# A hybrid layer and a 32-expert mixture on one core: TensorE's order in the expert loop fixed by issue edges, the last norm's weights loaded

## The chip, the cores and the metric

The kernel runs on one core of a Trainium2 chip. The time is device microseconds of one execution, from its start to its end; the time before is the median of three runs. One further execution was taken by the hardware profiler, and all rows below come from it. TensorE multiplies (PE: its matmuls, PEld: its weight loads), VectorE is DVE, ScalarE is ACT, GpSimd is POOL, and SyncE (SP) issues the transfers.

## The reference, cut to what matters

Two blocks over 256 tokens of width 1024. The first mixes four branches (three attentions and a convolution) and ends in a gated feed-forward; the second has a pooling and differential-attention mixer, cross attention and a mixture of experts. Only the last stage is touched by the change in more than a detail:

```python
def clamped_swiglu(gu):
    gate, up = gu[..., :D_EXPERT], gu[..., D_EXPERT:]
    gate = jnp.minimum(gate, SWIGLU_LIMIT)
    up = jnp.clip(up, -SWIGLU_LIMIT, SWIGLU_LIMIT)
    return (up + 1.0) * gate * jax.nn.sigmoid(SWIGLU_ALPHA * gate)

def moe_ffn(...):        # 256 tokens, 32 experts, each token to its best 4
    logits = (xt @ w_router + b_router).astype(jnp.float32)
    top_val, top_idx = lax.top_k(logits, TOP_K)
    gates = jax.nn.softmax(top_val, axis=-1)
    ...
        hb = clamped_swiglu(xb @ w_gu[e] + b_gu[e])    # w_gu[e]: 1024 x 2048
        yb = hb @ w_down[e] + b_down[e]                # w_down[e]: 1024 x 1024
        return yb * g[:, None].astype(yb.dtype)
    ...
    y = jnp.zeros((T, D), h.dtype).at[row_tok].add(...)

x = x + moe_ffn(rms_norm(x, ffn_norm_g[l]), ...)
return rms_norm(x, final_norm_g)
```

All is float32. Every expert's weights are read once: 8 MiB of `w_gu` and 4 MiB of `w_down`, 384 MiB in all.

## The kernel before

The first 750 us or so compute everything up to the router; the rest is a loop over 32 experts (`NE`), each with room for 64 tokens (`CAP`). An expert that got more tokens is finished by `overflow()`, a run-time branch (`tc.If`) whose body is skipped when no expert has more than 64.

**Slots.** The expert weights stream through 24 buffers of 128 x 2048 floats (`slot_tile()`, taken in turn). A slab is one transfer of 1 MiB into one slot: an expert has 8 slabs of gate/up weights (`load_gu`) and 4 of down weights (`load_dn`). All are issued on SP's queue in the order of use; a slot's next load waits until TensorE has used the slot, and also for an earlier transfer. The last slab of expert 31 comes in two halves.

**One expert on TensorE.** `front(e)` runs `gu_product`: the 64 gathered tokens times 8 slabs, into two PSUM banks (`gue`, tag mm, line 1513), 8 records a slab in the trace. `gu_out` copies them to `gs` (ScalarE, line 1521). `swiglu` turns `gs` in two halves, `make(0)` and `make(1)`, each 4 transposes (`gte`, line 1534) and then six operations on VectorE and one on ScalarE, into `u_`. `dn_product` multiplies `u_` by 4 slabs (`dne`, tag y, line 1560, 8 records a slab) and splits the sum into `yh` and `yl` (ScalarE line 209, VectorE line 210), scaled by the slot's gate. `slots_of` makes the one-hot tile `Se` on VectorE and turns it on TensorE (`ste`, lines 1432 and 1433) into `sT`. `scatter` adds the rows to the tokens' sums with 8 matmuls (`acc`, line 1570), which stay in four PSUM banks through the loop. Every second expert `gather` picks the tokens of the next two (`xgg`, line 1460, 32 records) with a selection tile `SXg` from VectorE, and VectorE copies them out (line 1462).

**The order.** The loop is skewed: in iteration e the gate/up product of e + 1 runs, then the down product of e. The small pieces are handed in as `between`, a table from k (the step of the product ahead of which the call stands) to functions. In `gu_product` k counts slabs, in `dn_product` half slabs. That position is only the place in the program text: a scheduler orders the instructions of each engine by their dependences, and may move small matmuls among the large ones. Edges of issue (`tc.issue_after`, wrapped in `behind`) forbid this where they are given; the products have none.

**The end.** `EOVER` is 29: in that iteration all weights of 30 and 31 that are left are issued, since SP's queue must not stop at the branch. Behind the branch (line 1607) stand the spreading of the last norm's weights over the partitions (`gb2`, 16 records of line 1669), the swiglu of expert 30, the products gate/up 31, down 30 and down 31, the last scatters, and `finish`, which scales and stores the result.

Of the kernel before, what the change touches and what calls it, by code (L numbers as in the profile page):

```python
# [22 lines left out]
P = 128  # L23
T = 256
D = 1024
# [18 lines left out]
def kernel(ctx: ExitStack, tc: tile.TileContext, A, out, probe=None, stop=None):  # L44
# [45 lines left out]
    def ps(name, tag="mm"):  # L90
        return pst["pool"].tile([P, 512], F32, tag=tag, name=name, bufs=pst["tags"][tag])
# [400 lines left out]
    def attention(name, qk, kchunk, vcol, bias, sink=None, extra=None, cq=None):  # L492
# [3 lines left out]
        for p in range(4):  # L496
# [36 lines left out]
            for j in range(2):  # L533
                ptr = ps(f"{name}t{p}{j}", "tr")
                for b in (1, 0):
# [3 lines left out]
                    for s in range(b + 1):  # L539
# [28 lines left out]
    v5 = load_vecs("v5", [("attn", r128(A["attn_norm_g_2"]), 8), ("xattn", r128(A["xattn_norm_g_2"]), 8),  # L568
                     ("memn", r128(A["mem_norm_g_2"]), 8), ("ffn", r128(A["ffn_norm_g_2"]), 8),
                     ("pscale", r128(A["pool_scale_2"]), 4), ("subln", A["subln_g_2"], 1),  # L570
                     ("fgattn", A["final_g"].rearrange("(c p) -> c p", p=P), 8),
                     ("last", A["final_norm_g_2"].rearrange("(c p) -> c p", p=P), 8)])


    qc = qk_group("foxqk", 1792, 8, 4)
# [916 lines left out]
    def load_gu(src, ahead=()):  # L1492
        return [*ahead, *(gu_piece(src, k, slot_tile()) for k in range(len(ahead), 8))].__getitem__
# [10 lines left out]
    def gu_product(wt, xg, col, name, between=None):  # L1504

        pgu = [ps(f"gu{name}_{n}") for n in range(2)]
        for k in range(8):
            for f in (between or {}).get(k, ()):
                f()
            w = wt(k)  # L1510
            for n in range(2):
                for cg in range(2):
                    PE.matmul(pgu[n][cg * CAP:(cg + 1) * CAP, :], xg[:, k, col:col + CAP],  # L1513
                              w[:, cg * D + n * 512:cg * D + (n + 1) * 512], start=k == 0, stop=k == 7)
        return pgu
# [35 lines left out]
    def dn_product(wt, gslot, name, u_=u_, tag="y", between=None):  # L1551

        po = ps(f"dn{name}", tag)
        for k in range(8):
            for f in (between or {}).get(k, ()):
                f()
            if k % 2 == 0:
                w = wt(k // 2)
            for cg in range(2):
                PE.matmul(po[cg * CAP:(cg + 1) * CAP, :], u_[:, k // 4, k % 4, :],  # L1560
                          w[:, k % 2, cg * 512:(cg + 1) * 512], start=k == 0, stop=k == 7)
        hilo(yh, yl, po, scale=gslot() if callable(gslot) else gslot)

    def scatter(stop=False, after=None):
# [20 lines left out]

    def front(e, between):
        w = load_gu(w_gu[e], () if e else gu0)
        pgu = gu_product(w, st["xg"], (e % GR) * CAP, f"e{e}", between)

        return gu_out(pgu, f"e{e}", slot_tile()[:, :D] if e == EOVER + 1 else None)  # L1590

    def slots_of(e):
        st["gslot", e] = turn_slots(one_hot(pos1[:, :, e:e + 1], 1, f"e{e}")[:, :, 0], gate3[:, :, e, :], f"e{e}")
# [8 lines left out]

    def overflow():
        wsl = [slot_tile() for _ in range(2)]
        oxg = slot_tile()[:, :D // 2].rearrange("p (c s) -> p c s", c=8)
# [29 lines left out]

    for e in range(NE - 2):
        make = swiglu(gs, bgu[:, :, e], f"e{e}")
        make(0)
        between = {1: [lambda: make(1, "y")], 4: [lambda: slots_of(e)]}
        if e and e - 1 != EOVER:  # L1640
            between[3] = [scatter]
        gs = front(e + 1, between)
        wd = load_dn(w_dn2[e])
        if e == 15:
            load_b_down()
        if e == EOVER:

            wg1 = load_gu(w_gu[e1])
            wd0, wd1 = load_dn(w_dn2[e0]), load_dn(w_dn2[e1], halves=True)
        if e == 2:  # L1650
            counts()
        between = {}
        if e % GR == 0:
            _, four = group(e // GR + 1)
            between = {0: [lambda: four(0)], 4: [lambda: four(1)]}
        if e == 15:
            between = {4: [gates_down], 6: [add_b_down]}
        dn_product(wd, st["gslot", e], f"e{e}", between=between)

    scatter()  # L1660
    overflow()


    work = slot_tile()
    gb2 = work[:, D:]
    for h in range(2):
        pt = ps(f"gb2_{h}")
        for c in range(4):
            PE.matmul(pt[:, c * P:(c + 1) * P], vec["last"][:, 4 * h + c:4 * h + c + 1].to_broadcast([P, P]), ident,  # L1669
                      start=True, stop=True)  # L1670
        S.copy(gb2[:, half(h)], pt)
    make = swiglu(gs, bgu[:, :, e0], f"e{e0}")
    make(0)
    slots_of(e0)
    gs = gu_out(gu_product(wg1, st["xg"], (e1 % GR) * CAP, f"e{e1}", {1: [lambda: make(1)]}), f"e{e1}")
    u1 = slot_tile()[:, :2 * 4 * CAP].rearrange("p (h c s) -> p h c s", h=2, c=4)
    make1 = swiglu(gs, bgu[:, :, e1], f"e{e1}", u1)
    dn_product(wd0, st["gslot", e0], f"e{e0}", between={2: [lambda: make1(0)], 4: [lambda: make1(1)]})
    dn_product(wd1, lambda: st["gslot", e1], f"e{e1}", u_=u1, tag="mm",
               between={2: [scatter], 4: [lambda: slots_of(e1)]})  # L1680
    ssl = mp.tile([P, 3, 2], F32, name="ssl")
# [49 lines left out]
```

## Time and profile before

| | |
|---|---|
| median of three runs | 1711.93 us (1711.44 to 1714.88) |
| the profiled execution | 1709.1 us |
| its span, first to last instruction | 1707.4 us |
| TensorE matmuls busy | 1621.0 us, 95% |
| weight loads / VectorE / ScalarE / GpSimd busy | 59% / 42% / 30% / 13% |
| read from HBM | 524.95 MB |

The page cuts the span into 40 slices of 42.7 us and gives each engine's busy share in tenths. A busy TensorE is not one at its peak, since matmuls overlap and their ends are modelled; how long a record takes in a run is better read from the starts of neighbouring rows in the timeline. A wait is put down to the event that ended it.

### The profile page before, as it was taken

The page shows a single profiled execution, that of the slowest core. Times are in us where ns is not written, and L with a number is a line of the kernel's source. Part 1 is how long each engine was busy: PE and PEld are TensorE (multiplying, and loading weights), DVE is VectorE, ACT ScalarE, POOL GpSimd, SP SyncE. Part 2 cuts the span into 40 slices and gives each one's busy share as a digit, 9 for nine tenths or more (in the row PEclk, how much of TensorE's full clock was granted, in tenths as well). Part 3 has the DMA queues.
Part 4 walks back from the last instruction along what each step waited for, and adds up shares of the span by engine and source line. Part 5 has one row for each costly group of instructions (what it writes and reads, how often), then busy time and mean ns, then how long its engine had stood idle before and what let it go on. Part 6 is the DMA issues. An engine that isn't in the chain of part 4 may idle for free. (4 is left out here: it accounts for less than half of the span.)

```text
span 1707.4 us, 23465 instructions
## 1 busy us (share of the span) xinstructions
PE 1621.0 (95%) x9269; PEld 1002.7 (59%) x9270; DVE 722.7 (42%) x1613; ACT 510.5 (30%) x959; POOL 221.2 (13%) x319
## 2 busy tenths in 40 slices
PE   9899999999999999999999999999999999999977
PEld 8887799989999888974333333333333333333332
DVE  5967654667777776542222212212121212122212
ACT  4465554555555555531110111001011110010101
POOL 6988412200011000000000000000000000000000
PEclk9999999999999999999999999999999999999988
DMA  9842355655554535689999999999999999999991
GB/s 293 256 161 71 103 185 185 225 188 183 192 188 161 187 121 182 258 341 411 421 421 420 421 421 421 420 421 421 410 421 421 422 420 421 421 421 421 421 417 63
DMA packets 166320, 527.60 MB, mean 309 GB/s; under 512 B 13617, under 2 KB 101598, under 8 KB 117150
## 3 DMA queue, kind: packets, MB, share of 16 engines
q1 hardware_dynamic: 166206, 526.06, 79.4%
q8 instruction: 74, 1.21, 0.3%
q14 instruction: 40, 0.33, 0.1%
HBM read 524.95 MB, written 4.22 MB: 310 GB/s over the span
## 5 line engine op out<-in xcount | busy, mean ns | idle before, releaser
L1513 PE MATMUL gue<-raw,xgg 128*64 128x512 f32 x2032 | 461.7, 598 | 0.0
L185 DVE TENSOR_TENSOR wl<-raw,wh 128x1024 fp32r<-128x1024 f32 (+3 forms) x218 | 273.6, 1256 | 177.7 <-ACT wh L184 177.0
L184 ACT CAST wh<-raw 128x1024 fp32r<-128x1024 f32 (+2 forms) x220 | 227.8, 1035 | 256.0 <-PE g L193 64.5
L1513 PEld LDWEIGHTS gue<-raw,xgg 128*64 128x64 f32 x2032 | 136.2, 136 | 255.5 <-issue 236.1
L1560 PE MATMUL dne<-raw,u__8509 128*64 128x512 f32 x992 | 236.0, 603 | 1.3 <-DVE u__8509 L1548 1.3
L1540 DVE TENSOR_TENSOR gse<-gte,bgu 128x256 f32<-128x256 f32 x62 | 26.3, 424 | 261.8 <-PE gte L1534 259.0
L1521 ACT COPY gse<-gue 128x512 f32<-128x512 f32 x62 | 36.3, 586 | 331.2 <-PE gue L1513 331.2
L1462 DVE TENSOR_TENSOR xgg<-xgg_h,v_c 128x512 f32<-128x512 f32 x30 | 20.7, 691 | 252.4 <-PE gue L1513 180.2
L1560 PEld LDWEIGHTS dne<-raw,u__8509 128*64 128x64 f32 x992 | 63.9, 136 | 102.7 <-issue 89.2
L1691 POOL TENSOR_TENSOR ssl<-ssl,nhalf 128x1 f32<-128x1 f32 x2 | 1.1, 556 | 947.1 <-DVE ssl L1690 947.1
L1546 ACT ACTIVATE gse<-gse 128x256 f32<-128x256 f32 x62 | 25.8, 417 | 265.7 <-DVE gse L1544 265.7
L1460 PEld LDWEIGHTS xgg_h<-SXg,x_t 128*128 128x128 f32 x480 | 57.9, 191 | 61.1 <-issue 26.0
L1460 PE MATMUL xgg_h<-SXg,x_t 128*128 128x128 f32 x480 | 69.0, 287 | 19.0 <-DVE xgg L1462 11.1
L379 POOL TENSOR_TENSOR convo<-convo,prod 128x256 f32<-128x256 f32 x90 | 76.9, 854 | 7.4
L192 PE MATMUL g<-h_h,wh 128*128 128x256 f32 x256 | 73.1, 286 | 0.0
L193 PE MATMUL g<-h_l,wh 128*128 128x256 f32 x256 | 73.1, 285 | 0.0
L194 PE MATMUL g<-h_h,wl 128*128 128x256 f32 x256 | 72.9, 285 | 0.0
L378 POOL TENSOR_SCALAR prod<-hconv,v_c 128x256 f32<-128x256 f32 x90 | 67.8, 753 | 8.6
L209 ACT ACTIVATE yh<-dne,gslote 128x512 fp32r<-128x512 f32 x32 | 22.0, 687 | 142.4 <-PE dne L1560 142.4
L210 DVE SCALAR_TENSOR_TENSOR yl<-dne,gslote,yh 128x512 fp32r<-128x512 f32 x32 | 24.0, 750 | 94.7 <-ACT yh L209 94.7
L1534 PEld LDWEIGHTS gte<-ident,gse 128*128 128x128 f32 x248 | 34.4, 207 | 50.3 <-issue 37.3
L1570 PE MATMUL acc<-yh,sT 64*128 64x512 f32 x128 | 34.5, 444 | 22.6 <-ACT yh L209 22.6
(807 smaller groups left out, 3092.5 us busy)
## 6 DMA issues: line engine op xcount, KB each, us to landing
raw<-in_w_gu_dram SPq DMA_DIRECT2D x254, 1024.0 KB
raw<-in_w_down_dram SPq DMA_DIRECT2D x138, 1024.0 KB
raw<-in_w_in_dram SPq DMA_DIRECT2D x32, 1024.0 KB
raw<-in_w_up_dram SPq DMA_DIRECT2D x22, 1024.0 KB
raw<-in_w_out_dram SPq DMA_DIRECT2D x8, 1024.0 KB
raw<-in_w_ckv_dram SPq DMA_DIRECT2D x8, 1024.0 KB
raw<-in_w_in_dram SPq DMA_DIRECT2D x13, 512.0 KB
raw<-in_w_br_dram SPq DMA_DIRECT2D x12, 512.0 KB
```

Source lines behind the costliest of these rows:

```text
L184: S.copy(hi, src)
L185: last["lo"] = (eng or V).tensor_sub(lo, src, hi.bitcast(F32))
L192: PE.matmul(o, wh[:, k, :], ah[:, k, :], start=first and k == 0, stop=False)
L193: PE.matmul(o, wh[:, k, :], al[:, k, :], start=False, stop=False)
L194: PE.matmul(o, wl[:, k, :], ah[:, k, :], start=False, stop=last and k == nk - 1)
L378: G.tensor_scalar(prod[0][:, :T], hconv[:, c, k:k + T], w, 0.0, op0=ALU.mult, op1=ALU.add)
L379: G.tensor_add(convo[:, c, :], convo[:, c, :], prod[0][:, :T])
L1460: PE.matmul(po[:, i * w:(i + 1) * w], x_t[:, b, (4 * h + i) * P:(4 * h + i + 1) * P], s_[:, b].rearrange("p o s -> p (o s)"), start=b == 0 ...
L1513: PE.matmul(pgu[n][cg * CAP:(cg + 1) * CAP, :], xg[:, k, col:col + CAP], w[:, cg * D + n * 512:cg * D + (n + 1) * 512], start=k == 0, stop ...
L1521: S.copy(gs[:, n * 512:(n + 1) * 512], pgu[n])
L1560: PE.matmul(po[cg * CAP:(cg + 1) * CAP, :], u_[:, k // 4, k % 4, :], w[:, k % 2, cg * 512:(cg + 1) * 512], start=k == 0, stop=k == 7)
L1570: PE.matmul(acc[b][h], sT[rows_, b * P:(b + 1) * P], y[rows_, :], start=False, stop=stop and y is yl)
```

## The change

- `gu_product` and `dn_product` note their last matmul, and what `between` hands in at step k is issued behind it (`behind(m)`).
- The two swiglu halves stand together, ahead of slab 2 of the next gate/up product; the scatter and the slot turn together, ahead of slab 5; the gather's two halves together in the middle of the down product, the second in a bank of tag mm. The one-hot tile is made by a call of its own, `hot(e)`, ahead of the product.
- The swiglu of expert 30 moves into the down product of expert 29, ahead of the branch. Its result and the overflow's gathered tile share the unused half of the slot that holds `gs` of 30 (`st["keep"]`).
- The last norm's weights are loaded over all partitions by one transfer (512 KB) issued behind the last expert's weights. The matmuls and copies that spread them, and the row that carried them in an early load, go.

```diff
@@ early loads
-                     ("fgattn", A["final_g"].rearrange("(c p) -> c p", p=P), 8),
-                     ("last", A["final_norm_g_2"].rearrange("(c p) -> c p", p=P), 8)])
+                     ("fgattn", A["final_g"].rearrange("(c p) -> c p", p=P), 8)])
@@ gu_product (dn_product alike)
+        m = {}
         for k in range(8):
-            for f in (between or {}).get(k, ()):
-                f()
+            with behind(m):
+                for f in (between or {}).get(k, ()):
+                    f()
...
-                    PE.matmul(pgu[n][cg * CAP:(cg + 1) * CAP, :], xg[:, k, col:col + CAP],
-                              w[:, cg * D + n * 512:cg * D + (n + 1) * 512], start=k == 0, stop=k == 7)
+                    m["P"] = PE.matmul(pgu[n][cg * CAP:(cg + 1) * CAP, :], xg[:, k, col:col + CAP],
+                                       w[:, cg * D + n * 512:cg * D + (n + 1) * 512], start=k == 0, stop=k == 7)
@@ the loop
-        make(0)
-        between = {1: [lambda: make(1, "y")], 4: [lambda: slots_of(e)]}
-        if e and e - 1 != EOVER:
-            between[3] = [scatter]
+        hot(e)
+
+        between = {2: [lambda: make(0), lambda: make(1, "y")], 5: [lambda: slots_of(e)]}
+        if e:
+            between[5].insert(0, scatter)
         gs = front(e + 1, between)
...
-            between = {0: [lambda: four(0)], 4: [lambda: four(1)]}
+            between = {4: [lambda: four(0), lambda: four(1, "mm")]}
...
+        if e == EOVER:
+
+            wg1 = load_gu(w_gu[e1])
+            wd0, wd1 = load_dn(w_dn2[e0]), load_dn(w_dn2[e1], halves=True)
+            work = slot_tile()
+            gb2 = work[:, D:]
+            ldc(gb2, A["final_norm_g_2"].unsqueeze(0).broadcast_to([P, D]))
+
+            u0 = st["keep"][:, D + D // 2:].rearrange("p (h c s) -> p h c s", h=2, c=4)
+            make0 = swiglu(gs, bgu[:, :, e0], f"e{e0}", u0)
+            between = {4: [lambda: make0(0), lambda: make0(1, "mm")]}
         dn_product(wd, st["gslot", e], f"e{e}", between=between)
@@ behind the branch
-    work = slot_tile()
-    gb2 = work[:, D:]
-    for h in range(2):
-        pt = ps(f"gb2_{h}")
-        for c in range(4):
-            PE.matmul(pt[:, c * P:(c + 1) * P], vec["last"][:, 4 * h + c:4 * h + c + 1].to_broadcast([P, P]), ident,
-                      start=True, stop=True)
-        S.copy(gb2[:, half(h)], pt)
-    make = swiglu(gs, bgu[:, :, e0], f"e{e0}")
-    make(0)
-    slots_of(e0)
-    gs = gu_out(gu_product(wg1, st["xg"], (e1 % GR) * CAP, f"e{e1}", {1: [lambda: make(1)]}), f"e{e1}")
+    hot(e0)
+    gs = gu_out(gu_product(wg1, st["xg"], (e1 % GR) * CAP, f"e{e1}", {4: [lambda: slots_of(e0)]}), f"e{e1}")
...
-    dn_product(wd0, st["gslot", e0], f"e{e0}", between={2: [lambda: make1(0)], 4: [lambda: make1(1)]})
+    hot(e1)
+    dn_product(wd0, st["gslot", e0], f"e{e0}", u_=u0, between={4: [lambda: make1(0), lambda: make1(1, "mm")]})
```

TensorE in the loop, before: the gate/up product of expert 14 (`gue14`, two banks) with the second swiglu half of 13 (`gte13`) and the scatter of 12 (`acc`) among its first slabs:

```order
L1513 MATMUL gue14_0_10420<-raw509_10404,xgg7_10352 64x512 x2
L1513 MATMUL gue14_1_10421<-raw509_10404,xgg7_10352 64x512 x2
L1534 MATMUL gte13_1_10426<-ident_76,gse13_10336 128x128 x4
L1570 MATMUL acc00_8478<-yl_8507,sT_8508 128x512
L1570 MATMUL acc01_8479<-yl_8507,sT_8508 128x512
L1570 MATMUL acc11_8481<-yh_8506,sT_8508 128x512
L1570 MATMUL acc10_8480<-yl_8507,sT_8508 128x512
L1513 MATMUL gue14_0_10420<-raw510_10406,xgg7_10352 64x512 x2
L1513 MATMUL gue14_1_10421<-raw510_10406,xgg7_10352 64x512 x2
L1570 MATMUL acc11_8481<-yl_8507,sT_8508 128x512
L1513 MATMUL gue14_0_10420<-raw511_10408,xgg7_10352 64x512 x2
L1513 MATMUL gue14_1_10421<-raw511_10408,xgg7_10352 64x512 x2
```

The same product after, from its second slab to the start of the scatter:

```order
L1514 MATMUL gue14_0_10410<-raw510_10396,xgg7_10351 64x512 x2
L1514 MATMUL gue14_1_10411<-raw510_10396,xgg7_10351 64x512 x2
L1535 MATMUL gte13_0_10420<-ident_76,gse13_10335 128x128 x4
L1535 MATMUL gte13_1_10432<-ident_76,gse13_10335 128x128 x4
L1514 MATMUL gue14_0_10410<-raw511_10398,xgg7_10351 64x512 x2
L1514 MATMUL gue14_1_10411<-raw511_10398,xgg7_10351 64x512 x2
L1514 MATMUL gue14_0_10410<-raw512_10400,xgg7_10351 64x512 x2
L1514 MATMUL gue14_1_10411<-raw512_10400,xgg7_10351 64x512 x2
L1514 MATMUL gue14_0_10410<-raw513_10402,xgg7_10351 64x512 x2
L1514 MATMUL gue14_1_10411<-raw513_10402,xgg7_10351 64x512 x2
L1573 MATMUL acc00_8477<-yh_8505,sT_8507 128x512
L1573 MATMUL acc01_8478<-yh_8505,sT_8507 128x512
```

Both swiglu halves now stand in one run behind the second slab, and the whole scatter behind the fifth.

TensorE in the down product of expert 14 (`dne14`), before: the end of the gather for experts 16 and 17 (`xgg8`) and the first swiglu half of 15 (`gte15`), with one slab between each and the next:

```order
L1460 MATMUL xgg8_h1_10644<-SXg8_10619,x_t_107 128x128 x3
L1560 MATMUL dne14_10625<-raw529_10611,u__8509 64x512 x4
L1460 MATMUL xgg8_h1_10644<-SXg8_10619,x_t_107 128x128 x5
L1560 MATMUL dne14_10625<-raw530_10613,u__8509 64x512 x4
L1534 MATMUL gte15_0_10664<-ident_76,gse15_10608 128x128 x4
L1560 MATMUL dne14_10625<-raw531_10615,u__8509 64x512 x4
```

After:

```order
L1563 MATMUL dne14_10624<-raw529_10610,u__8508 64x512 x4
L1563 MATMUL dne14_10624<-raw530_10612,u__8508 64x512 x4
L1459 MATMUL xgg8_h0_10633<-SXg8_10618,x_t_107 128x128 x8
L1459 MATMUL xgg8_h1_10643<-SXg8_10618,x_t_107 128x128 x8
L1563 MATMUL dne14_10624<-raw531_10614,u__8508 64x512 x4
L1563 MATMUL dne14_10624<-raw532_10616,u__8508 64x512 x4
```

The gather is one run in the middle, and the swiglu half has gone to the next product.

TensorE behind the overflow branch, before: the spreading of the norm's weights (`gb2`) and the first swiglu half of 30 are followed by its slot turn, and the down product of 30 starts:

```order
L1607 UNCONDITIONAL_BRANCH
L1669 MATMUL gb2_0_13238<-ident_76,v5_c_2353 128x128 x4
L1669 MATMUL gb2_1_13244<-ident_76,v5_c_2353 128x128 x4
L1534 MATMUL gte30_0_13250<-ident_76,raw710_12674 128x128 x4
L1432 LDWEIGHTS Se30_13262
```

After:

```order
L1615 UNCONDITIONAL_BRANCH
L1514 MATMUL gue31_0_13264<-raw715_12684,xgg15_12540 64x512 x2
L1514 MATMUL gue31_1_13265<-raw715_12684,xgg15_12540 64x512 x2
L1514 MATMUL gue31_0_13264<-raw716_12686,xgg15_12540 64x512 x2
L1514 MATMUL gue31_1_13265<-raw716_12686,xgg15_12540 64x512 x2
```

The gate/up product of 31 is now the first thing behind the branch.

## Rows read from the trace of the kernel before

**Rows 1.** The page's span, TensorE's slices (tenths busy) and the transfers' rate.

```profile
span 1707.4 us, 23465 instructions
PE   9899999999999999999999999999999999999977
GB/s 293 256 161 71 103 185 185 225 188 183 192 188 161 187 121 182 258 341 411 421 421 420 421 421 421 420 421 421 410 421 421 422 420 421 421 421 421 421 417 63
```

**Rows 2.** TensorE's timeline, one pair of experts: start, us, engine, line, what, count.

```profile
1301.26 0.73 PE L1570 MATMUL acc<-yh,sT 64*128 64x512 f32 x3 [0.79 <-ACT yh L209]
...
1308.16 0.71 PE L1460 MATMUL xgg_h<-SXg,x_t 128*128 128x128 f32 x4 [0.66 <-DVE gslote L1436]
1308.80 1.94 PE L1513 MATMUL gue<-raw,xgg 128*64 128x512 f32 x8
1310.67 1.60 PE L1460 MATMUL xgg_h<-SXg,x_t 128*128 128x128 f32 x12
1312.20 8.80 PE L1513 MATMUL gue<-raw,xgg 128*64 128x512 f32 x40
...
1339.39 10.52 PE L1513 MATMUL gue<-raw,xgg 128*64 128x512 f32 x48
1349.84 0.74 PE L1534 MATMUL gte<-ident,gse 128*128 128x128 f32 x4
...
1359.37 0.73 PE L1570 MATMUL acc<-yh,sT 64*128 64x512 f32 x3 [0.79 <-ACT yh L209]
```

**Rows 3.** TensorE's matmul waits, 820 to 1640 us: total, times, longest.

```profile
PE acc L1570 <- ACT yh L209: 21.0, 27, 0.8
PE xgg_h L1460 <- DVE xgg L1462: 11.1, 14, 0.8
PE xgg_h L1460 <- DVE gslote L1436: 7.9, 12, 0.7
PE ste L1432 <- DVE u__8509 L1542: 6.3, 12, 0.5
```

**Rows 4.** The waits of its weight loads, 820 to 1640 us, those for transfers.

```profile
PEld gue L1513 <- DMA raw<-in_w_gu_dram: 8.3, 27, 0.4
...
PEld gue L1513 <- DMA raw<-in_w_down_dram: 6.0, 20, 0.4
```

**Rows 5.** SP's timeline, the issues of the last weights.

```profile
1614.93 17.73 SPq L1480 DMA_DIRECT2D raw<-in_w_gu_dram  x8
...
1652.21 3.31 SPq L1500 DMA_DIRECT2D raw<-in_w_down_dram  x2
```

**Rows 6.** Windows: stretch, length, busy by engine, PE's granted clock, DMA share, GB/s.

```profile
40.00:70.00 30.00, 25.28 (x135) 23.06 (x133) 29.52 (x44) 13.74 (x22) 27.35 (x32) 1.00 0.91 269
...
1652.20:1659.00 6.80, 3.00 (x14) 3.03 (x15) 0.49 (x2) 0.00 (x0) 0.00 (x0) 0.50 1.02 417
1671.00:1673.30 2.30, 2.30 (x12) 0.70 (x10) 0.00 (x0) 0.00 (x0) 0.00 (x0) 1.00 0.12 43
```

**Rows 7.** TensorE's timeline, from expert 29's down product to the last one.

```profile
1640.24 7.04 PE L1560 MATMUL dne<-raw,u__8509 128*64 128x512 f32 x32
...
1656.00 3.45 PE L1669 MATMUL gb<-ident,v_c 128*128 128x128 f32 x16 [6.42 <-PEq L1607]
...
1662.35 1.94 PE L1560 MATMUL dne<-raw,u__8509 128*64 128x512 f32 x2 [1.26 <-DVE u__8509 L1548]
...
1689.64 0.50 PE L1570 MATMUL acc<-yh,sT 64*128 64x512 f32 x2
...
1690.78 1.94 PE L1560 MATMUL dne<-raw,raw 128*64 128x512 f32 x8
1692.65 0.23 PE L1432 MATMUL ste<-ident_b,Se 128*128 128x128 bf16 x1
...
1692.90 3.65 PE L1560 MATMUL dne<-raw,raw 128*64 128x512 f32 x16
```

**Rows 8.** The page's group of a swiglu operation: count, busy us, mean ns, idle before.

```profile
L1540 DVE TENSOR_TENSOR gse<-gte,bgu 128x256 f32<-128x256 f32 x62 | 26.3, 424 | 261.8 <-PE gte L1534 259.0
```

More of the change, by code (lines that the diff above doesn't have):

```diff
@@ L1553, in dn_product @@
         po = ps(f"dn{name}", tag)
+        m = {}
         for k in range(8):
-            for f in (between or {}).get(k, ()):
-                f()
+            with behind(m):
+                for f in (between or {}).get(k, ()):
+                    f()
             if k % 2 == 0:
@@ L1559, in dn_product @@
             for cg in range(2):
-                PE.matmul(po[cg * CAP:(cg + 1) * CAP, :], u_[:, k // 4, k % 4, :],
-                          w[:, k % 2, cg * 512:(cg + 1) * 512], start=k == 0, stop=k == 7)
+                m["P"] = PE.matmul(po[cg * CAP:(cg + 1) * CAP, :], u_[:, k // 4, k % 4, :],
+                                   w[:, k % 2, cg * 512:(cg + 1) * 512], start=k == 0, stop=k == 7)
         hilo(yh, yl, po, scale=gslot() if callable(gslot) else gslot)
@@ L1587, in front, with hot @@
         w = load_gu(w_gu[e], () if e else gu0)
+        if e == EOVER + 1:
+            st["keep"] = slot_tile()
         pgu = gu_product(w, st["xg"], (e % GR) * CAP, f"e{e}", between)
-        return gu_out(pgu, f"e{e}", slot_tile()[:, :D] if e == EOVER + 1 else None)
+        return gu_out(pgu, f"e{e}", st["keep"][:, :D] if e == EOVER + 1 else None)
+    def hot(e):
+        st["hot"] = one_hot(pos1[:, :, e:e + 1], 1, f"e{e}")[:, :, 0]
     def slots_of(e):
-        st["gslot", e] = turn_slots(one_hot(pos1[:, :, e:e + 1], 1, f"e{e}")[:, :, 0], gate3[:, :, e, :], f"e{e}")
+        st["gslot", e] = turn_slots(st["hot"], gate3[:, :, e, :], f"e{e}")
     chunk, _ = group(0)
@@ L1604, in overflow @@
         wsl = [slot_tile() for _ in range(2)]
-        oxg = slot_tile()[:, :D // 2].rearrange("p (c s) -> p c s", c=8)
+        oxg = st["keep"][:, D:D + D // 2].rearrange("p (c s) -> p c s", c=8)
         most = nc.values_load(cnt_i[0:1, NE:NE + 1], min_val=0, max_val=T)
@@ L1645 @@
             load_b_down()
-        if e == EOVER:
-            wg1 = load_gu(w_gu[e1])
-            wd0, wd1 = load_dn(w_dn2[e0]), load_dn(w_dn2[e1], halves=True)
         if e == 2:
@@ L1661 @@
     overflow()
-    work = slot_tile()
-    gb2 = work[:, D:]
-    for h in range(2):
-        pt = ps(f"gb2_{h}")
-        for c in range(4):
-            PE.matmul(pt[:, c * P:(c + 1) * P], vec["last"][:, 4 * h + c:4 * h + c + 1].to_broadcast([P, P]), ident,
-                      start=True, stop=True)
-        S.copy(gb2[:, half(h)], pt)
-    make = swiglu(gs, bgu[:, :, e0], f"e{e0}")
-    make(0)
-    slots_of(e0)
-    gs = gu_out(gu_product(wg1, st["xg"], (e1 % GR) * CAP, f"e{e1}", {1: [lambda: make(1)]}), f"e{e1}")
-    u1 = slot_tile()[:, :2 * 4 * CAP].rearrange("p (h c s) -> p h c s", h=2, c=4)
+    hot(e0)
+    gs = gu_out(gu_product(wg1, st["xg"], (e1 % GR) * CAP, f"e{e1}", {4: [lambda: slots_of(e0)]}), f"e{e1}")
+    u1 = work[:, :2 * 4 * CAP].rearrange("p (h c s) -> p h c s", h=2, c=4)
     make1 = swiglu(gs, bgu[:, :, e1], f"e{e1}", u1)
-    dn_product(wd0, st["gslot", e0], f"e{e0}", between={2: [lambda: make1(0)], 4: [lambda: make1(1)]})
+    hot(e1)
+    dn_product(wd0, st["gslot", e0], f"e{e0}", u_=u0, between={4: [lambda: make1(0), lambda: make1(1, "mm")]})
     dn_product(wd1, lambda: st["gslot", e1], f"e{e1}", u_=u1, tag="mm",
```

## The prediction

> **What bounds the kernel now.** I read four views in this order: the page's slices, the waits of TensorE in the expert loop, its timeline over one pair of experts, and the timelines of the last 100 us. In the slices the second half of the run looks like two engines at their limit at once: TensorE is at 9 tenths or more and the transfers stand at 421 GB/s in nearly every slice [rows 1]. Only one of them can set the end. The waits say which: between 820 and 1640 us TensorE's weight loads waited for transfers for 8.3 and 6.0 us in pieces of at most 0.4 us [rows 4], while matmuls waited for 21.0 + 11.1 + 7.9 + 6.3 = 46.3 us on ScalarE and VectorE [rows 3]. So the weights lie there before they are used, and **TensorE runs at its own pace**: from one scatter to the same scatter two experts later 1301.26 to 1359.37, 58.1 us, 29.05 an expert [rows 2]. The transfers need less than they get: an expert is 12 slabs of 1.05 MB, 12.6 MB / 421 GB/s = 29.9 us. The two rates are close, but TensorE started late and is still behind at the end: the final weights have landed by 1673.3 (43 GB/s in the last 2.3 us) [rows 6], and TensorE starts the last product only at 1692.90 [rows 7].
>
> How far behind? Take the last slab of w_down of expert 29, the last one before the overflow branch. TensorE starts its product at 1640.24, 24 records of 0.2145 us before the last slab, so it reaches that one at 1645.4 [rows 7]. Behind this slab 16 more come (gate/up of 31, down of 30 and 31): 16.8 MB / 421 = 39.9 us, counted back from 1673.3 gives 1633.4 for the slowest of the DMA engines, and some 4 us less for the mean one. I take **1632.7** (bounds 1629 to 1633.4), nearest to the slowest, since a slab is whole only with it. TensorE is then 12.7 us late there, after 30 experts. **Each expert has only to become 12.7 / 30 = 0.42 us cheaper, 28.6 instead of 29.05, and TensorE stands at the weights' heels; what is saved beyond that is worth nothing.**
>
> **Part 1, the runs.** Prices from one pair [rows 2]. 48 records of the gate/up product took 10.45 (1339.39 to 1349.84), 8 took 1.87 (1308.80 to 1310.67): 0.2145 a record and 0.154 at each end of a run. 12 gather records took 1.53 and 4 took 0.64: 0.111 each and 0.195 a run. Before, the products of a pair are interrupted 13 times in the timeline, five of them with a wait of 0.5 to 0.8 [rows 3]; after, 5 times: two runs of 8 transposes, two of scatter plus slot turn, one of 32 gather records. Cost after: products 192 x 0.2145 + 5 x 0.154 = 41.95; transposes 2 x (0.195 + 8 x 0.111) = 2.17; the scatter in the order that after uses everywhere took 1.14 in the last expert (1689.64 to 1690.78), the slot turn 0.25 (1692.65 to 1692.90) [rows 7], twice 1.39 = 2.78; gathers 0.195 + 32 x 0.111 = 3.75. Sum **50.65 a pair, 25.3 an expert**, from 29.05. If no run end were saved and only the waits on ScalarE and VectorE went, it would be 46.3 us over some 28 experts less, 27.4. If something were lost, it is a new wait: the swiglu now begins after slab 2 of the next gate/up product, and its 12 VectorE operations of at most 0.424 [rows 8] and two of ScalarE lie under the 6 slabs left, 6 x 1.72 = 10.3 us. The gather's second bank is one of the gate/up pair, and its copies have had two slabs (3.4 us) of the down product. The gathered tile must be copied out under the last two slabs, again 3.4 us. So the bounds are 25.3 to 27.4, both under 28.6, and **this part is worth 12.7 us at that slab**, whatever its exact size. The one-hot tile is now made earlier on VectorE, which is mostly idle there; nothing, since the slot turn needs it 10 us later.
>
> **Part 2, the branch.** From the last slab of expert 29 to the first matmul behind the branch it took 1656.00 - 1645.4 = 10.6 us, 6.42 of it a wait on TensorE's own sequencer at the branch [rows 7]. The change leaves the branch's body nearly as it is; I keep the 10.6. Unknown: bounds 7 to 13, by the wait that could halve or grow by a third. Restart 1632.7 + 10.6 = 1643.3.
>
> **Part 3, behind the branch.** Before, from 1656.00 to the last 4 records of the last product (1692.90 + 12 x 0.2145 = 1695.5) is 39.5 us [rows 7]. The 16 records that spread the last norm's weights take the first 3.3 of it; swiglu 30 and the wait for it end at 1662.35 [rows 7]. After, gate/up 31 can start at once, since swiglu 30 lies ahead of the branch. Its cost: 64 x 0.2145 + 2 x 0.154 + slot turn 0.25 = 14.3; down 30 with the 8 transposes 32 x 0.2145 + 0.31 + 1.08 = 8.25; down 31 up to its last 4 records 28 x 0.2145 + 0.31 + 1.14 + 0.25 = 7.7. [...] Sum 14.3 + 8.25 + 7.7 + 1.5 = **31.75, 7.7 less than before**. Last 4 records at 1643.3 + 31.75 = 1675.05. They need the last half slab, at 1673.3: met, with 1.75 us in hand, so that the transfers are the floor just below (1685.2 for the span).
>
> **Part 4, the loaded norm weights.** One more transfer of 512 KB on SP's queue, behind all weights: the last half slabs are issued by 1655.5 [rows 5]. 0.52 MB / 421 = 1.25 us, landed by about 1675, and wanted by the final multiply, which stands behind the last records, the split of their sums on ScalarE and VectorE and the last scatter. Hidden; without that cover it costs 1 to 2.5. SP then reaches the branch 1 to 2.5 us later, and nothing waits on SP there but the output, 20 us on. The 4 KB row that is no longer loaded early, its 8 transposed columns, and one weight transfer that moves a place in SP's queue there: 0, at most one transfer of 1.05 MB, 2.5, either way. In the first experts SP waits for free slots; a faster TensorE frees them earlier, 0 to 2 us for the whole stream. I take 0.5.
>
> **Sum.** Last 4 records 1675.05 - 0.5 = 1674.6 against 1695.5: the span is 1707.4 - 20.9 = **1686.5**. The profiled execution took 1709.1, 1.7 over its span, and the median of the runs is 1711.9; the same 20.9 off gives **1691.0**. Terms: 12.7 catching up, 7.7 behind the branch, 0.5 stream.
>
> **The rivals.** *Only the tail gains.* The run ends were not what made the pair long, or the waits come back at other places, and an expert stays above 28.6. Then 7.7 is left: 1704.2. Against it stands that the 46.3 us of waits alone are 3.6 times what is needed. 0.08.
>
> *A wait eats all*, such as the gather's copy held up by VectorE ahead of the next product, by 3.6 us an expert, or the order isn't what the diff says. The instruction order shows the regrouping; time 1711 to 1713. 0.04.
>
> *The clock gives way, slower.* TensorE that keeps up with the transfers must wait: 25.3 of every 29.9 us busy, 85%. [...] Against it: from 40 to 70 us TensorE was busy 25.28 of 30 us, 84%, and was granted 1.00 throughout; 0.50 appears after the 6.42 us at the branch [rows 6, 7]. 0.04. [...]
>
> **How the numbers follow.** Forecast 0.84, the rivals 0.08, 0.04, 0.04. Its range: landing -3.7 to +0.7, branch -3.6 to +2.4, clock -1.5 to +1.9, stream -1.5 to +3, norm load up to +2.5. Downward the floor of the transfers stops it at -1.3 and the stream may move that by -1.5 to -3 more; upward I add the likelier half, +7.5. So **1686.5 to 1698.5**. It leaves out the rivals' 0.16 and little else. Faster than 1708.5 (0.2%, about what can be told from no change): 0.84 + 0.08 = 0.92; same 0.04; slower 0.04.
>
> **What would show it.** Right: waits of TensorE for transfers grow from 14 us to over 50 in the loop, the last third above all; 421 GB/s stays flat to about 1670; a pair takes 51 us early and 59.8 later; the last slab of expert 29 is used near 1633; 32 us from the restart to the last 4 records. Wrong: a pair above 57, clock 0.50 inside the loop, slices under 421 GB/s, or a restart later than 1646.

## The result, and the profile after

| | before | after |
|---|---|---|
| median of the runs | 1712.12 us (1711.44 to 1714.88, 4 runs) | 1693.81 us (1691.35 to 1695.98, 4 runs) |
| ratio | | 0.989 (0.987 to 0.991) |
| the profiled execution | 1709.1 us | 1691.35 us |
| its span | 1707.4 us | 1689.7 us |

1691.0 was predicted, with 1686.5 to 1698.5 as the range. Most of the steps came out as written; one term, the moment at which the weights land, was 3 us off, and most of that goes with something that the prediction had not looked at.

The page after (beside [rows 1]; PEclk is the granted clock in tenths):

```profile
span 1689.7 us, 23460 instructions
PE   8899999999999999999999999898998899889877
PEclk9999999999999999999999999999999999999999
GB/s 283 264 170 63 113 177 180 209 188 218 165 182 193 175 132 174 250 319 382 418 421 418 420 419 419 419 420 419 410 419 419 420 419 420 419 420 418 420 418 287
```

In the second half TensorE is no longer at 9 tenths everywhere, and the transfers are flat to the last slice but one: the two have changed places. TensorE's matmul waits from 820 to 1640 us say the same (beside [rows 3]), and those of its weight loads (beside [rows 4]):

```profile
PE dne L1563 <- DMA raw<-in_w_down_dram: 32.1, 56, 1.5
PE gue L1514 <- DMA raw<-in_w_gu_dram: 25.5, 46, 0.7
PE acc L1573 <- ACT yh L209: 0.8, 1, 0.8
...
PEld gue L1514 <- DMA raw<-in_w_gu_dram: 85.9, 88, 1.6
...
PEld dne L1563 <- DMA raw<-in_w_down_dram: 40.5, 30, 2.4
```

Of the 46.3 us of waits on ScalarE and VectorE 0.8 are left; in their place stand 57.6 us in which matmuls waited for weights. (The weight loads waited 126.4 us for them, where it was 14.3 before.) TensorE's timeline shows how it came to that (beside [rows 2]): the same run in three early experts, then in two experts of a later pair, with two slabs between them.

```profile
814.60 5.37 PE L1514 MATMUL gue<-raw,xgg 128*64 128x512 f32 x24
...
838.03 5.37 PE L1514 MATMUL gue<-raw,xgg 128*64 128x512 f32 x24
...
865.68 5.37 PE L1514 MATMUL gue<-raw,xgg 128*64 128x512 f32 x24
...
1253.98 5.60 PE L1514 MATMUL gue<-raw,xgg 128*64 128x512 f32 x24
...
1270.11 1.94 PE L1563 MATMUL dne<-raw,u__8508 128*64 128x512 f32 x8 [0.47 <-DMA raw<-in_w_down_dram]
1272.69 1.94 PE L1563 MATMUL dne<-raw,u__8508 128*64 128x512 f32 x8 [0.65 <-DMA raw<-in_w_down_dram]
...
1313.84 5.58 PE L1514 MATMUL gue<-raw,xgg 128*64 128x512 f32 x24
```

The early pair takes 865.68 - 814.60 = 51.08 us, the later one 1313.84 - 1253.98 = 59.86: from about 1045 us on TensorE waits for about every second slab (from there to 1640 us 102 waits, 0.56 us each on the mean). The end (beside [rows 7]) and SP's last issue (beside [rows 5]):

```profile
1633.79 3.90 PE L1563 MATMUL dne<-raw,u__8508 128*64 128x512 f32 x16
...
1646.30 8.53 PE L1514 MATMUL gue<-raw,xgg 128*64 128x512 f32 x32 [6.31 <-PEq L1615]
...
1655.00 7.09 PE L1514 MATMUL gue<-raw,xgg 128*64 128x512 f32 x32
1661.92 3.60 PE L1563 MATMUL dne<-raw,raw 128*64 128x512 f32 x16
...
1675.15 3.65 PE L1563 MATMUL dne<-raw,raw 128*64 128x512 f32 x16
```

```profile
1662.27 0.33 SPq L1669 DMA_DIRECT2D raw<-in_final_norm_g_dram  x1
```

The last slab of expert 29 is used at 1635.76 (the first row holds the last two slabs and takes 0.25 longer than in a run, a wait between them), TensorE restarts behind the branch at 1646.30, and the last four records start at 1675.15 + 12 x 0.2145 = 1677.7. Windows of the same execution (beside [rows 6]; the clock is the last but two of the numbers):

```profile
1642.40:1649.20 6.80, 2.90 (x8) 1.11 (x10) 0.49 (x2) 0.00 (x0) 0.00 (x0) 0.50 1.03 418
...
1400.00:1600.00 200.00, 178.67 (x876) 65.20 (x875) 41.54 (x129) 20.77 (x41) 0.00 (x0) 1.00 1.01 419
...
1674.00:1676.00 2.00, 2.00 (x14) 0.63 (x12) 0.16 (x1) 0.37 (x1) 0.00 (x0) 1.00 0.62 248
1676.00:1677.50 1.50, 1.50 (x10) 0.57 (x8) 0.00 (x0) 0.00 (x0) 0.00 (x0) 1.00 0.17 68
1677.50:1679.00 1.50, 1.31 (x8) 0.14 (x2) 0.00 (x0) 0.14 (x1) 0.00 (x0) 1.00 0.02 8
```

The weights run out between 1676 and 1677.5 (the last half slab's signal came at 1677.2), half a microsecond ahead of the records that need them. Up to the branch TensorE waits for transfers; behind it its own records follow each other without a wait, and the last landing stands just below them. **The transfers set the time up to the branch now, and are the floor behind it.** In the loop they run at 419 GB/s, not at the 421 of before.

### The profile page after: what moved, and what is told of

Same layout as the page of the kernel before. It is cut to its first block, busy times and chain, and to the rows that moved or that the text cites. A ratio compares the mean times of both kernels' runs of the same rounds, so it can differ in the third digit from the quotient of the medians.

```text
span 1689.7 us, 23460 instructions
## 1 busy us (share of the span) xinstructions
PE 1592.4 (94%) x9253; PEld 990.3 (59%) x9254; DVE 713.1 (42%) x1613; ACT 510.2 (30%) x957; POOL 221.6 (13%) x319
## 5 line engine op out<-in xcount | busy, mean ns | idle before, releaser
L1514 PE MATMUL gue<-raw,xgg 128*64 128x512 f32 x2032 | 473.0, 602 | 32.0 <-DMA raw<-in_w_gu_dram 25.5
L1563 PE MATMUL dne<-raw,u__8508 128*64 128x512 f32 x960 | 226.8, 602 | 32.1 <-DMA raw<-in_w_down_dram 32.1
L1414 DVE TENSOR_TENSOR Se<-iota_s,pos 128x128 bf16<-128x128 f32 x64 | 15.9, 288 | 119.8 <-PE ste L1432 113.0
L1459 PE MATMUL xgg_h<-SXg,x_t 128*128 128x128 f32 x480 | 57.6, 278 | 0.0
L1433 ACT CAST sT<-ste 128x256 fp32r<-128x256 f32 x32 | 11.9, 373 | 148.6 <-PE ste L1432 148.6
```

The source lines that it names most:

```text
L1459: PE.matmul(po[:, i * w:(i + 1) * w], x_t[:, b, (4 * h + i) * P:(4 * h + i + 1) * P], s_[:, b].rearrange("p o s -> p (o s)"), start=b == 0 ...
L1514: m["P"] = PE.matmul(pgu[n][cg * CAP:(cg + 1) * CAP, :], xg[:, k, col:col + CAP], w[:, cg * D + n * 512:cg * D + (n + 1) * 512], start=k = ...
L1563: m["P"] = PE.matmul(po[cg * CAP:(cg + 1) * CAP, :], u_[:, k // 4, k % 4, :], w[:, k % 2, cg * 512:(cg + 1) * 512], start=k == 0, stop=k == 7)
```

## The experiments

Twelve kernels, each beside runs of the kernel before on the same chip, which had a median of 1712.83, 1712.68 and 1713.64 us beside the first, second and last four. The theory at the start: the loop's regrouping brings TensorE to the weights' heels (12.7 us), the shorter end brings 7.7, and the transfers are the floor. Its rivals: the order in the loop is worth little and the end does it all; or what TensorE does is not what sets the time.

**The change again**, for the spread and for the rate.

> The changed kernel once more, beside the next three. Theory (TensorE keeps up with the transfers from the first third of the loop on, so the end is the transfers' end plus some 12 us): 1693.8 us again, a pair of experts at 51 us before about 1045 us and at 59.8 behind it. If 421 GB/s in the profile of before against 419 to 420 here was a matter of one execution, this one may show either; if it is a matter of the order, 419 to 420 again.

1693.58 us (1691.42 to 1694.41), ratio 0.9884 (0.9870 to 0.9898), 419 GB/s again. So the lower rate was no accident of one execution.

**Without the edges.** The pieces keep their new places in the program, but nothing forbids the scheduler to move them:

```diff
-            with behind(m):
-                for f in (between or {}).get(k, ()):
-                    f()
+            for f in (between or {}).get(k, ()):
+                f()
```

> The changed kernel without the issue edges in both products: the small pieces stand at the new places in the text, but the scheduler may move them; the tail is the new one. Theory (the edges make the runs, and only cheaper experts let TensorE catch up): experts stay near 29 us, TensorE never waits for transfers in the loop, and only the part behind the branch is left, 7.7 to 8 us: 1704 us. Rival (the new places in the text are enough): 1694 us.

1696.85 us (1694.65 to 1698.4), between the two. The scheduler did put the small pieces back among the slabs, and TensorE never waited for a transfer in the loop; but a pair took 57.5 us, not 58.1. That was against the theory as it stood. The one wait that had gone was that of the gather on VectorE's copy, 11.1 us in [rows 3]. The only thing that could have removed it was the bank: the gather's second half no longer uses the bank of its first. The next two kernels follow this up.

**The end alone**: x_noedge, and in the loop before's places and before's bank:

```diff
-        hot(e)
-        between = {2: [lambda: make(0), lambda: make(1, "y")], 5: [lambda: slots_of(e)]}
-        if e:
-            between[5].insert(0, scatter)
+        make(0)
+        between = {1: [lambda: make(1, "y")], 4: [lambda: hot(e), lambda: slots_of(e)]}
+        if e:
+            between[3] = [scatter]
...
-            between = {4: [lambda: four(0), lambda: four(1, "mm")]}
+            between = {0: [lambda: four(0)], 4: [lambda: four(1)]}
```

> Only the end of the change: the swiglu of expert 30 ahead of the branch, the last norm's weights loaded, nothing done by TensorE behind the branch but the products; in the loop all small pieces stand where they stood before, with no issue edges, and the gather keeps its bank. Theory (the loop's gain comes from the small pieces' places and edges, the tail is worth 7.7 us by itself): a pair of experts stays at 58.1 us, 29.05 an expert, waits for transfers in the loop stay near 14 us, the branch is reached as late as before, the last four records come 32 instead of 39.5 us after the restart: 1712.8 - 7.7 = 1705. Rival (a part of the tail, such as the one-hot tile by a call of its own or one slot less in use, speeds the loop too): an expert at 28.7 or less, 1697 or below.

1706.39 us (1705.06 to 1706.7), ratio 0.9961 (0.9947 to 0.9975). Its end on TensorE:

```profile
1644.93 7.09 PE L1561 MATMUL dne<-raw,u__8508 128*64 128x512 f32 x32
...
1660.66 9.23 PE L1513 MATMUL gue<-raw,xgg 128*64 128x512 f32 x32 [6.33 <-DMA raw<-in_w_down_dram]
...
1690.22 3.65 PE L1561 MATMUL dne<-raw,raw 128*64 128x512 f32 x16
```

The restart is at 1660.66 there, the last four records start at 1690.22 + 2.57 = 1692.8: 32.1 us instead of 39.5, as expected. What the end is worth is 6.3, not 7.7: the swiglu of 30 has not vanished, its 8 transposes (1.5 us) now lie ahead of the branch.

**The bank alone added to that:**

```diff
-            between = {0: [lambda: four(0)], 4: [lambda: four(1)]}
+            between = {0: [lambda: four(0)], 4: [lambda: four(1, "mm")]}
```

> x_tail and one thing more: the second half of the gather takes a bank of the gate/up pair instead of the one that its first half uses. Theory from x_noedge, whose gather ran without its 0.79 us wait on VectorE: this bank alone makes the pair 57.5 instead of 58.1 us, 0.3 us an expert, 9 us over 30 experts, so that the time falls from x_tail's 1705 to about 1697. Rival (in x_noedge it was the new places in the program, not the bank): the wait on xgg stays, 58.1 a pair, 1705.

1697.42 us (1697.31 to 1698.58). Waits of x_tail (first row), then of x_bank; then the expert with a gather in x_tail, from one scatter to the next, and a pair of x_bank:

```profile
PE xgg_h L1459 <- DVE xgg L1461: 11.1, 14, 0.8
```

```profile
PE acc L1571 <- ACT yh L209: 21.0, 27, 0.8
PE ste L1431 <- DVE u__8508 L1542: 13.7, 26, 0.5
PE xgg_h L1459 <- DVE gslote L1435: 7.9, 12, 0.7
```

```profile
1304.38 0.73 PE L1571 MATMUL acc<-yh,sT 64*128 64x512 f32 x3 [0.79 <-ACT yh L209]
...
1336.35 0.73 PE L1571 MATMUL acc<-yh,sT 64*128 64x512 f32 x3 [0.79 <-ACT yh L209]
```

```profile
1299.94 0.73 PE L1571 MATMUL acc<-yh,sT 64*128 64x512 f32 x3 [0.79 <-ACT yh L209]
...
1331.27 0.73 PE L1571 MATMUL acc<-yh,sT 64*128 64x512 f32 x3 [0.79 <-ACT yh L209]
...
1357.42 0.73 PE L1571 MATMUL acc<-yh,sT 64*128 64x512 f32 x3 [0.79 <-ACT yh L209]
```

The wait on the copy is gone, but two thirds of it came back as a wait of the slot turn (6.3 to 13.7 us). An expert with a gather takes 31.33 instead of 31.97 us, 0.64 less; some 0.27 of that is waiting, and the rest came with the order, in which the down product is now broken twice and not three times. A pair takes 57.48 us, 0.31 less an expert, and 29 experts x 0.31 = 9.0 us: the 9.0 between 1706.4 and 1697.4. **One word, the bank, is half of the whole gain.** The runs and edges bring the other 3.6, from 1697.4 to 1693.8, and then the transfers stop it. The new places without the edges (x_noedge, 1696.85) add to the bank 0.6, which the spread doesn't tell from nothing.

**The loop alone**, with before's end, the early row of the norm's weights included:

```diff
+                     ("last", A["final_norm_g_2"].rearrange("(c p) -> c p", p=P), 8)])
...
-            ldc(gb2, A["final_norm_g_2"].unsqueeze(0).broadcast_to([P, D]))
...
-            between = {4: [lambda: make0(0), lambda: make0(1, "mm")]}
...
+            PE.matmul(pt[:, c * P:(c + 1) * P], vec["last"][:, 4 * h + c:4 * h + c + 1].to_broadcast([P, P]), ident,
...
+    make = swiglu(gs, bgu[:, :, e0], f"e{e0}")
+    make(0)
+    hot(e0)
+    slots_of(e0)
...
-    dn_product(wd0, st["gslot", e0], f"e{e0}", u_=u0, between={4: [lambda: make1(0), lambda: make1(1, "mm")]})
+    dn_product(wd0, st["gslot", e0], f"e{e0}", between={2: [lambda: make1(0)], 4: [lambda: make1(1)]})
```

> The changed loop with the old tail: swiglu 30 and the spreading of the last norm's weights by TensorE behind the branch. Theory: the last slab of expert 29 is used at the same time as in the changed kernel, and the part behind the branch takes 39.5 us instead of 31.4: 1693.8 + 8.1 = 1702 us. Rival (the transfers end so late that the old tail hides under them): 1694 to 1696 us.

1695.28 us (1693.24 to 1697.57), ratio 0.9902 (0.9888 to 0.9916). Here the expectation failed by 7: with the old end the time is only 1.7 above x_again, the rival's number. Its restart and its last product:

```profile
1642.40 3.75 PE L1679 MATMUL gb<-ident,v_c 128*128 128x128 f32 x16 [6.37 <-PEq L1616]
...
1677.04 3.65 PE L1564 MATMUL dne<-raw,raw 128*64 128x512 f32 x16
```

From the restart to the last four records it is 37.2 us, 5.8 more than in after; but the restart came 3.9 us earlier. Its weights came at 421 GB/s, and its stream had begun some 1.1 us earlier too (363.4 MB of weights were left at 800 us, 363.8 in after). So the old end isn't hidden: it costs its 5.8 us, and 3.9 came back from the transfers. The gains of loop and end don't add (17.5 and 6.3 alone, 19 together), and here the two kernels differ in the rate as well.

**Without the overflow branch** (the code that would finish an expert with over 64 tokens is left out; no expert has so many):

```diff
     scatter()
-    overflow()
```

> The changed kernel without the overflow branch, so an expert with more than 64 tokens would lose some. [...] Rival (the 6.3 us wait at the branch and the low clock behind it are on the path): 6 to 8 us less, 1686 to 1688 us.

1689.86 us (1687.66 to 1693.72), 3.7 below x_again, where at most 1 was expected, with the transfers as the floor. TensorE goes from expert 29 to 31 with no break and then waits for slabs:

```profile
1644.19 5.37 PE L1514 MATMUL gue<-raw,xgg 128*64 128x512 f32 x24
1649.95 1.94 PE L1514 MATMUL gue<-raw,xgg 128*64 128x512 f32 x8 [0.38 <-DMA raw<-in_w_gu_dram]
```

With 10.5 us taken off TensorE's path, 3.7 come out at the end, and not all of them need come from the branch: this kernel's weights came at 421 GB/s, which x_align below takes up. The floor is that close.

**Why 419 GB/s?** The rate was the open point: 421 in before, x_runs and x_nobranch, 419.4 in the rest. (x_nobranch loads the norm's weights by one transfer and runs at 421; the next expectation overlooks it.) Two kernels take the norm's weights apart from everything else. Before with that part alone changed:

```diff
-                     ("last", A["final_norm_g_2"].rearrange("(c p) -> c p", p=P), 8)])
...
     work = slot_tile()
     gb2 = work[:, D:]
-    for h in range(2):
...
-        S.copy(gb2[:, half(h)], pt)
+    ldc(gb2, A["final_norm_g_2"].unsqueeze(0).broadcast_to([P, D]))
```

> The kernel before with one part of the change alone: the last norm's weights are loaded over all partitions by one transfer instead of being spread by 16 matmuls of TensorE behind the branch. Theory: TensorE is what the end waits for, so 3.3 of the 39.5 us behind the branch go, 1709.5. Rival (the first records behind the branch are slow whatever they are, the clock there being at 0.50): the next piece takes the time over, 1712. What it also tells: whether this transfer is what lowers the rate of the whole stream. Profiles of kernels with it have shown 419.4 GB/s from 800 to 1600 us, those without it 421; if it is the cause, 419.4 here too.

1707.9 us (1705.55 to 1709.46), ratio 0.9969 (0.996 to 0.9979), 4.8 below its before where some 3 were expected, at 419.4 GB/s, although the new transfer starts there only behind the branch. And after with that part alone undone (the 16 matmuls ahead of gate/up 31):

```diff
+                     ("last", A["final_norm_g_2"].rearrange("(c p) -> c p", p=P), 8)])
...
-            ldc(gb2, A["final_norm_g_2"].unsqueeze(0).broadcast_to([P, D]))
...
+    for h in range(2):
...
+        S.copy(gb2[:, half(h)], pt)
     hot(e0)
```

> The changed kernel with that part alone undone: the last norm's weights are spread by 16 matmuls behind the branch, as before, all else as in the change. Theory (the rate of the stream has nothing to do with this transfer, and TensorE reaches the last half slab 0.5 to 2.4 us after it lands): the 3.3 us are added nearly whole, 1693.6 + 3 = 1696.5, with 419.4 GB/s. Rival (the transfer costs the stream 0.4 per cent, some 3.5 us by the end): 421 GB/s, the last slab of expert 29 lands 3.5 us earlier, and the two cancel: 1693 to 1694.

1693.08 us (1692.96 to 1695.49), ratio 0.9891 (0.9874 to 0.9907), at 421. TensorE spends 3.68 us on the spreading, and the time is that of after:

```profile
1645.28 3.75 PE L1683 MATMUL gb<-ident,v_c 128*128 128x128 f32 x16 [6.48 <-PEq L1616]
1648.96 7.30 PE L1515 MATMUL gue<-raw,xgg 128*64 128x512 f32 x32
```

So the rate goes with the norm's row, but a transfer at 1675 can't slow one at 800. What else goes with it is an address: that row had 8 of the columns of a table, 32 bytes a partition, and without them all 24 slots start 32 bytes lower, at 13600 and 97824 instead of 13632 and 97856. Every kernel so far with the first pair had run at 419.4, every one with the second at 421 (and x_nobranch, with 13600 and 97696). The test puts the 32 bytes back, unused:

```diff
-        ct = (pool or const).tile([P, n], F32, name=f"{name}_c", bufs=1)
+        ct = (pool or const).tile([P, n + 8 * (name == "v5")], F32, name=f"{name}_c", bufs=1)
```

> The changed kernel with 32 unused bytes a partition put back where the last norm's row stood, so that the 24 slots start at 13632 and 97856 bytes as in the kernel before instead of 13600 and 97824; nothing else differs. Theory (the slots' place, moved by 32 bytes when the row went, costs the stream its 0.4 per cent): 421 GB/s from 800 to 1600 us instead of 419.4, the last half slab lands near 1674 instead of 1677 to 1678.5, and since the last slab of expert 29 lands that much earlier too, TensorE restarts behind the branch 3.3 us earlier: 1693.6 - 3.3 = 1690.3. Rival (the load of the norm's weights, or the program's size, is what lowers the rate): 419.4 GB/s and 1693.6.

A window of it beside the same one of after above:

```profile
1400.00:1600.00 200.00, 178.45 (x878) 65.28 (x876) 41.54 (x129) 20.77 (x41) 0.00 (x0) 1.00 1.01 421
```

**The rate goes with the 32 bytes.** They move every tile behind that table, the slots among them; the stream writes only to slots, so I take their place to be the cause. A record of 8192 bytes took 312 ns most often instead of 313. The time did not move as expected: 1693.08 us (1692.61 to 1693.76), ratio 0.9887 (0.987 to 0.9905) against x_again's 0.9884, where 3.3 us were expected. In its profiled execution the stream had begun late: 365.2 MB of weights were left at 800 us against 363.8 in after, 29.5 against 29.3 at 1600, so it had made good some 2.7 us on the way. TensorE's clock had been granted at 0.98 in its first 200 us and 0.99 in the next 300, where after had 1.00. No median shows the gain. An estimate from the profiles: with each one's lead or lag at 800 us taken off, the last slab of expert 29 was used 2.6 to 2.9 us earlier than in after in the four kernels with this loop at 421 (x_runs, x_nonorm, x_align, x_align_bd), and 0.7 us later in x_again at 419.4.

**The down bias from another queue**, on top of x_align:

```diff
-            ld(bd["t"][h * NE:(h + 1) * NE, :512], A["b_down_2"][0, :, half(h)])
+            nc.scalar.dma_start(bd["t"][h * NE:(h + 1) * NE, :512], A["b_down_2"][0, :, half(h)])
```

> x_align and one thing more: the two 64 KB loads of the down bias, which stand between the weights on SP's queue near 1200 us, are issued by ScalarE. Theory: the stretch 1195 to 1215 keeps 421 GB/s instead of about 410, TensorE doesn't wait 1.5 us for that bias and isn't granted 0.50 behind it, the stream ends 0.5 to 1 us earlier: 1689.5. Rival (the bytes of those two loads take the same time from any queue): as x_align, 1690.3.

1690.83 us (1689.97 to 1692.03), ratio 0.9876 (0.9855 to 0.9897): the fastest that does everything, 2.2 below x_align. The stretch did not keep 421: from 1195 to 1215 us it moved 410 GB/s, x_align 403, which is 0.14 MB or 0.3 us. The longest wait there was 1.07 us instead of 2.03, and the clock was 1.00 in both. The profiled execution had also begun its stream 2.8 us earlier (364.0 MB left at 800). The two intervals of the ratio overlap, so how much of the 2.2 is the queue stays open.

**The threshold.** Idle matmuls ahead of each expert's transposes, 5 or 11:

```diff
+            if h == 0 and name[0] == "e":
+                for _ in range(5):
+                    PE.matmul(pt, ident, x_t[:, 0, half(0)], start=True, stop=True)
```

> The changed kernel with 5 idle matmuls of 512 columns ahead of each expert's swiglu transposes on TensorE, 5 x 0.43 = 2.15 us an expert: 27.4 instead of 25.3, which is what an expert would cost had the run ends brought nothing. Theory (28.6 is the threshold, below it all is the same): TensorE still catches up with the transfers, later than the 1045 us of the change, and the time moves only by the one pad that stands behind the branch, 1693.6 + 2 = 1695.6. Rival (every microsecond of an expert counts): 1693.6 + 60 = 1750 or more.

> The same with 11 idle matmuls, 4.7 us an expert: 30.0, above the threshold of 28.6. Theory: TensorE never catches up; it waits for transfers as little as before; an expert at 30.0 against 29.05 of before puts the last slab of expert 29 at about 1645 + 28 = 1673, restart 1684, last four records 31.4 + 4.7 later at 1720: 1734. Rival (the slack against transfers is larger than worked out): under 1710.

1741.11 us (1740.04 to 1742.35) and 1907.48 (1906.13 to 1908.14): both expectations missed, since the pads were twice as long as planned. Two records stand for one matmul here. x_pad5, a pair's two ends and the branch, then x_pad11:

```profile
1303.93 5.37 PE L1514 MATMUL gue<-raw,xgg 128*64 128x512 f32 x24
...
1326.21 4.56 PE L1535 MATMUL gte<-x_t,ident 128*128 128x512 f32 x10
1330.61 1.11 PE L1538 MATMUL gte<-ident,gse 128*128 128x128 f32 x8
...
1363.28 5.37 PE L1514 MATMUL gue<-raw,xgg 128*64 128x512 f32 x24
...
1690.60 9.22 PE L1514 MATMUL gue<-raw,xgg 128*64 128x512 f32 x32 [3.76 <-PEq L1618]
```

```profile
1313.80 9.71 PE L1535 MATMUL gte<-x_t,ident 128*128 128x512 f32 x22
1323.34 1.11 PE L1538 MATMUL gte<-ident,gse 128*128 128x128 f32 x8
```

Two views that the price of the branch rests on (part 2 below): a window around it in x_pad5, with 10 GB/s in its last column, and, from `--dma` on after, 1640 to 1646.3 us, what the queues of instructions moved (packets, MB, share):

```profile
1686.00:1691.00 5.00, 1.19 (x8) 0.62 (x8) 0.54 (x3) 0.00 (x0) 0.00 (x0) 0.71 0.03 10
```

```profile
q8 instruction: 1, 0.02, 1.1%
q14 instruction: 2, 0.02, 0.6%
```

The pads took 4.40 and 9.54 us an expert. Both kernels lie above the threshold, and neither waited for a transfer between 820 and 1640 us. From one to the other 32 x 5.14 = 164.5 us of work were added and 166.4 of time measured: above the threshold every microsecond counts. From after to x_pad5 32 x 4.40 = 140.8 were added and 47.3 measured, so 93.5 us, 2.9 an expert, cost nothing: 25.5 + 2.9 = 28.4 us is where the cover ended by this estimate, and 28.6 was predicted. That this holds from below wasn't tried with a smaller pad.

## Why the prediction was right, and where not

- **What bounds the kernel.** Right, that TensorE's own pace did, and that the transfers stand right behind. The threshold of 28.6 us an expert came out of the pads as 28.4.
- **Part 1, the runs.** A pair was priced at 50.65 early and 59.8 later and took 51.08 and 59.86; the waits for transfers grew to 57.6 us where over 50 were named (not in the last third above all, but from 1045 on; the 14 that it started from were waits of weight loads, and those grew to 126.4). What the working did not single out is the bank: of the 12.6 us between x_tail and after it alone gave 9.0, some 3.7 of them waits net of what came back, the rest one break fewer in the down product. The long runs are worth 3.5 us an expert as priced, and nearly all of that ended as waiting.
- **Part 2, the branch.** 10.6 kept, 10.54 measured (1635.76 to 1646.30). The bound of 7 below had a cause that no row of before showed: with the transfers nearly idle, in both padded kernels, the wait was 3.76 and 3.71 us instead of 6.31. So some 2.6 us of it go with the stream. In the wait at the branch of after, 1640 to 1646.3 us, the instruction queues moved three packets, where the 40 us ahead of it had one; in that of before, 1649.6 to 1656 us, they moved three as well. That TensorE waits for just these packets isn't shown.
- **Part 3, behind the branch.** 31.75 predicted, 31.42 measured (1646.30 to 1677.72), the low clock included: 0.50 from 1642.4 to 1649.2, 2.9 us of it behind the restart. The 1.5 us that stand in the sum for this clock are the author's estimate, and no run shows them as a time of their own; in after the first 32 records behind the restart took 8.53 us and the next 32, with 1.00 granted, 7.09, which is 1.44 less. As a gain it was over-sized: the step "swiglu 30 lies ahead of the branch" took its time out of one place and did not put it into the other. In x_tail, where nothing hides it, the end is worth 6.3 instead of 7.7.
- **Part 4, the norm's weights.** This is the term that failed. "The 4 KB row that is no longer loaded early" was put at "0, at most one transfer ... either way". Its transfer is worth nothing, but its 32 bytes moved the slots, and the stream lost 0.4 per cent. Counted in the transfers' records, after lagged before by 1.4 us at 800 us (363.8 MB of weights left against 363.2) and by 4.1 us at 1600 (29.3 against 27.6): 2.6 us came with the rate, the rest was there before the loop had got going. The last slab of expert 29 was used 3.1 us later than predicted (1635.76 against 1632.7); that the rate is the larger part of this is an estimate, and x_align, at 421 again, used that slab no earlier, at 1636.16, since it had begun later still. This part saves TensorE 3.7 us behind the branch and gives back about as much in the stream; the ratio of after without it is 0.9891 against 0.989. The loaded weights landed at 1678.5 instead of 1675, still ahead of the final multiply at 1681.
- **The sum.** Last four records 1677.7 instead of 1674.6, span 1689.7 instead of 1686.5, median 1693.8 instead of 1691.0: the same 3 us all along, within the range, whose bound for the landing (0.7 late) was too narrow but stood beside others. Three of the four signs of being wrong that the prediction named came, each by little: slices of 418 to 420 GB/s, a restart at 1646.30, and one fall of the clock inside the loop.
- **The rivals.** Only the tail gains: x_tail shows what that would have been, 1706.4 where 1704.2 was worked out. The clock did not give way: TensorE was busy 89% of the time from 1400 to 1600 us, with 39 waits for slabs of at most 0.7 us, and was granted 1.00 there. It fell to 0.50 once in the loop, for 7 us from 1215.7, behind a wait of 1.51 us for a slab of down weights near the loads of the down bias; in x_runs a longer wait at the same place was not followed by a fall (1.00 from 800 to 1600), so the length of the wait alone doesn't tell. The two waits, after's first:

```profile
1213.90 1.07 PE L1563 MATMUL dne<-raw,u__8508 128*64 128x512 f32 x2 [1.51 <-DMA raw<-in_w_down_dram]
```

```profile
1211.94 1.07 PE L1564 MATMUL dne<-raw,u__8509 128*64 128x512 f32 x2 [2.17 <-DMA raw<-in_w_down_dram]
```

Behind shorter waits the trace of after shows no fall: from 1222.6 to 1640 us TensorE's matmuls waited 71 times for a transfer, at most 0.7 us each, and the clock was 1.00 throughout.

## What to carry to other kernels

Work out at which pace the bottleneck changes hands, and price only the part of a gain above that; then look for the cheapest edit that gets most of the way, which here was a second bank for one gather. When an edit removes or adds a small buffer, compare the addresses of the large ones that follow it, and the transfer rate before and after, and not only the instructions. A term set to zero, as the 4 KB row was, deserves the question what else hangs on it.

## What the hardware showed that was not expected

- Slots 32 bytes lower cost 0.4 per cent of the rate from HBM (421 to 419.4 GB/s; 312 to 313 ns a record), in six kernels against five, and it came back with 32 unused bytes. Lower is not slower as such: x_nobranch, with its slots at 13600 and 97696, had 421 too. Which places are fast wasn't tried further.
- At the skipped branch TensorE waited 3.7 us with the transfers nearly idle (10 GB/s and less, in the two padded kernels) and 6.3 to 6.6 with 410 to 420 GB/s under way.
- Executions of one kernel differ by some 6 us with the clock granted on the mean: runs of the kernel before took 1708.92 to 1709.24 at 0.994 and 1715.2 to 1715.44 at 0.989. In the profiles part of it lies far ahead of the loop: the five executions whose clock was 1.00 up to 500 us had 363.2 to 364.4 MB of weights left at 800 us, the nine with stretches at 0.50 there 364.2 to 366.6, up to 8 us of the stream.
